# The 31-row convolution of one core's decoder step in 16 parts of 512 instead of 8 of 1024

## The chip, the core and the metric

The kernel runs on one core of a Trainium2 chip. The core has five engines that follow lists of instructions of their own and wait for each other by semaphores: TensorE (PE, with its weight loads shown apart as PEld), VectorE (DVE), ScalarE (ACT), GpSimd (POOL) and SyncE (SP), which here only issues transfers. [...] The metric is the time of one execution on the device in microseconds (us), as a median of runs.

## What is computed

Two layers of a decoder trunk for a prompt of 2048 tokens and 8 single-step samples, D_MODEL = 1024. The change lies in the even layer's branch A, a causal depthwise convolution of 31 rows over 512 channels, which follows a gated product of the input projection:

```python
def causal_depthwise_conv(x, buf, w):
    k_len, ch = w.shape
    xp = jnp.concatenate([buf.astype(x.dtype), x], axis=1)
    y = lax.conv_general_dilated(xp, w.astype(x.dtype)[:, None, :], window_strides=(1,), padding='VALID',
                                 dimension_numbers=('NWC', 'WIO', 'NWC'), feature_group_count=ch)
    return y, xp[:, xp.shape[1] - (k_len - 1):]
...
    p = h @ w_in
    glu_val, glu_gate, gate_a, qkv, z, beta_l, a_l = jnp.split(p, EVEN_SPLITS, axis=-1)
    c, conv_buf_new = causal_depthwise_conv(glu_val * jax.nn.sigmoid(glu_gate), conv_buf, dw_w)
    c = jax.nn.silu(layer_norm(c + dw_b.astype(c.dtype), ln_g, ln_b))
    a_out = c * jax.nn.silu(gate_a)
    qkv_c, qkv_buf_new = causal_depthwise_conv(qkv, qkv_buf, sc_w)
```

Branch B, a gated delta rule over q, k and v (with a short convolution of 4 rows), the output projections, memory cross attention and a second layer follow.

## The kernel before, in words

The kernel's text is a Python program that writes out the instructions of all engines in one order. The class `Flow` keeps a rough clock for each engine and for each piece of data; every wrapper (`F.mm` L160, `F.act` L176, `F.tt` L214, `F.stt` L218) adds a price to its engine's clock and issues the instruction. A dense generator makes TensorE's work; after each of its small steps `pump` lets side tasks take a step when their data are ready by the clocks (L336). `spawn` gives a task a rank: 2 for what dense work waits for soon, 1 for what it waits for later. A task of rank 1 is held back while ScalarE's or VectorE's clock is more than 3500 ns ahead of TensorE's (`LIM`, L60). The order on each engine is thus fixed before the run, by prices and not by events; an engine takes its instructions strictly in that order.

`phase1` (L650) is the input projection of the even layer. Its main part, `dense_main` (L938), takes 26 blocks of 128 output channels against five tiles of tokens (512, 512, 512, 260 and 260 columns). A group is one block against one tile: 24 matmuls into one of three PSUM banks of the pool `mm2`, then `fin_...` empties the bank. For the convolution's channels b = 0..3 a pair of blocks is run side by side: `fin_gate` (L852) writes tanh of the gate into the tile `glu` (ScalarE), `fin_val` (L862) multiplies it by the values (VectorE reads `glu` and PSUM). The blocks of q, k and v come between (`fin_qkv` L899: ScalarE empties the bank into `raw`; `conv4` L920: ScalarE makes the first product, VectorE three further ones, `qacc`, all in SBUF). The weights of a block come in two halves by SP's queue and are split into `rhi` (ScalarE or VectorE) and `rlo` (GpSimd or VectorE, by `F.ve` L207) ahead of their use; the last four blocks are z 3 and the gates sg 0..3.

`conv31` (L877) is the convolution of one half of one channel block: ScalarE makes the first product with the bias into `cacc` [128, 1024] in SBUF, VectorE adds 30 products in place, one instruction of 1024 elements a partition each (L886), two at a step. There are 8 such parts; `conv_q` lets two be open at a time and `cacc` has two places. The part is stored to DRAM by SP's queue. `dense_main` starts the gate of channel block b only when all of b - 2 is convolved (L943).

`tail` (L958) waits for the last q, k, v convolution, starts `sample_mix` (L2068, the samples' own convolutions and delta steps, rank 2, whose small matmuls go into banks of the pool `bg2`, five banks given out in turn under one tag), and when the 8 parts and the mix are done it closes their places. `places` (L1382) opens the delta rule's places once that and the second token tile of the last three blocks (`h1`) are done; then `prep` (L1102) loads the first chunks of k, q and decays. The delta rule's chain over 16 chunks follows, with products of the attention weights (`Fill`) as dense work, and then the rest of the two layers.

Of the kernel before, what the change touches and what calls it, by code (L numbers as in the profile page):

```python
# [30 lines left out]
class Pool:  # L31
    """A tile pool that notes whose place each tile takes."""
# [23 lines left out]
class Flow:  # L56
    """Engine wrappers that keep rough clocks of the engines and of the data, and the interleaving of side tasks with
    dense work by these clocks."""

    LIM = (1500.0, 3500.0, 1e9)  # L60
    # what passes from the end of an operation till another one sees its result
    VIS = {"pe": 130.0, "act": 190.0, "dve": 130.0, "pool": 110.0}

    def __init__(self, nc, tc):
        self.nc, self.tc = nc, tc
        self.rel = {}
        self.t = {"pe": 0.0, "act": 0.0, "dve": 0.0, "pool": 0.0, "sync": 0.0, "gpsimd": 0.0, "scalar": 0.0}
        self.hw = self.ring = 0.0
        self.tick, self.cold, self.cols = 0, True, 0.0
        self.cur = self.t0 = 0.0  # L70
        self.tasks = []
        # by tensor: writes and reads as (first, last partition, first, last element, time), last use, free place
        self.wr, self.rd, self.last, self.slot = {}, {}, {}, {}
        # stores that wait for their data before they join their queue: by tensor, time and arguments
        self.pend = {}
# [13 lines left out]
    def region(ap):  # L89
        a, o = ap.ap, ap.offset  # L90
        n = ap.tensor.name
        if ap.space == DRAM or a[0][0] == 0:
            # (writes to DRAM never meet earlier ones here)
            return n, -1, 1, o, o + sum((c - 1) * abs(s) for s, c in a)
# [12 lines left out]
    def ready(self, ins, outs, eng):  # L107
# [3 lines left out]
        for r in outs:  # L111
# [3 lines left out]
            # products on the same place of PSUM follow each other without a wait  # L115
# [32 lines left out]
    def pe_op(self, cost, out, lhsT, rhs):  # L148
        """the array's clock halves after a tick with too little work"""
# [38 lines left out]
    def move(self, out, in_, scale=None):  # L188
        """copy on whichever of ScalarE and VectorE is free first"""
# [8 lines left out]
    def rows(self, out, in_, f):  # L198
        """out[:, h, :] = in_[:, h, :] * f[:, h], on whichever of ScalarE and VectorE ends first"""
# [7 lines left out]
    def ve(self, n, w=0.0):  # L207
        """VectorE or GpSimdE for an operation on n elements a partition, whichever ends first"""
# [55 lines left out]
    def dma(self, out, in_, eng="sync"):  # L264
        """a transfer; it joins its queue, where each waits for the ones before it, only when its data and place are ready"""
# [41 lines left out]
    def split(self, hi, lo, src, eng="dve", scale=1.0):  # L307
        """hi + lo == src, both in float32r."""
# [4 lines left out]
    def spawn(self, gen, hi=1, front=False):  # L313
        """hi: 2 what dense work waits for soon, 1 what it waits for later, 0 what may wait"""
# [34 lines left out]
    def until(self, cond):  # L349
        """dense work: let side tasks go on till cond holds"""  # L350
# [7 lines left out]
    def run(self, dense=None):  # L358
        """Alternate dense quanta (generator) with side-task steps until the dense work ends."""
# [42 lines left out]
def rsqrt(F, pool, y, x, n, tag, eng="dve"):  # L402
    """y = x ** -0.5 on a narrow float32 tile [128, n]."""
# [11 lines left out]
def token_rstd(F, C, pool, ppool, acc, n, scale, tag):  # L415
    """acc [128, n] holds partial sums; returns [128, nc] of (sum over partitions * scale + eps) ** -0.5,
    tokens on partitions."""
# [11 lines left out]
def spread(F, C, pool, ppool, r, n, tag, dg=None):  # L429
    """r [128, nc] tokens on partitions -> psum [128, n], every partition holding the row of tokens."""  # L430
# [15 lines left out]
def mm3_steps(F, out, K, w, x):  # L446
    """generator: out += (w0 + w1)^T (x0 + x1) without the product of the two low parts."""
# [21 lines left out]
class Ring:  # L469
    """Weight blocks [128, width] in two float32r parts, in n places that are taken in turn; they are loaded in parts of  # L470
    lw columns."""

    def __init__(self, F, pool, n, raw, width=1024, lw=512, tag="r"):
# [6 lines left out]
        # where the places lie, as [pool, number], and the ring that had the first ones  # L480
        self.where, self.prev = [[pool, n]], None
        # a second pool for the parts as they come, as (pool, number, up to which block)
# [6 lines left out]
    def has(self, name, i):  # L489
        """the block is in place by the clocks"""  # L490
# [10 lines left out]
    def place(self, i):  # L501
        """the pool of a block and its places"""
# [16 lines left out]
    def load(self):  # L519
        """the next part of a block"""  # L520
# [69 lines left out]
def bc(ap, n):  # L590
    """[128, k] -> [128, k, n] with the last axis repeated"""
# [4 lines left out]
def gates(F, C, cp, tp, bgp, D, st):  # L596
    """generator: per token and head beta, the cumulated log decay in its chunk, and its exponentials"""
# [16 lines left out]
    # softplus(x) = max(x, 0) + log1p(exp(-|x|))  # L614
# [8 lines left out]
    # log1p(e) = ln(u) + (e - (u - 1)) / u  # L623
# [26 lines left out]
def phase1(F, C, I, D, st, P, R, mmp, bgp, loaders, mix, hp):  # L650
    """Input projection of the even layer with its two causal convolutions. R: the weights' places; loaders: what loads
    them, and after them the weights of what follows; mix(pool): the sample tokens. The places of h are given back
    tile by tile: the first one's, hp, are taken by what follows."""
# [7 lines left out]
    def hs(t, x, k):  # L661
        """part x of h: channels k of token tile t"""
        return h0[8 * x + k] if t == 0 else ht[t][x][:, k, :]

    # (the gates of the first half, which nothing else waits for, come last)
# [22 lines left out]
    # token tiles: x -> h, beside the memory keys and values of the first layer  # L688
    with F.tile_pool(name="x1", bufs=1, side="right") as xp:
        R.more = xp, NMORE, 33  # L690
        # the last token tile's place holds the memory till its own h comes
# [37 lines left out]
        def squares():  # L729
            """adds up the squares of each token"""  # L730
# [74 lines left out]
        def ba(t, w):  # L805
            """beta and the decays before their functions, tokens on partitions"""
# [42 lines left out]
    conv_q, cdone, qdone = Res(2), set(), set()  # L849
# [12 lines left out]
    def fin_val(b, t, n, ps):  # L862
# [6 lines left out]
        if t == 1:  # L869
            F.spawn(conv31(b, 0))  # L870
        if t == 4:
# [3 lines left out]
            F.spawn(conv31(b, 1))  # L875

    def conv31(b, u):  # L877
        yield conv_q.ok
        conv_q.take()
        g = gl[b]  # L880
        acc = ap.tile([128, 1024], F32, tag="cacc", name="cacc", bufs=2)
        o = 1024 * u
        F.act(acc, g[:, o:o + 1024], AF.Identity, scale=C.dww[:, b, 0:1], bias=C.dwb[:, b:b + 1])
        yield
        for i in range(1, 31):
            F.stt(acc, g[:, o + i:o + i + 1024], C.dww[:, b, i:i + 1], acc, ALU.mult, ALU.add)  # L886
            if i % 2 == 0:
                yield
        F.dma(D.c[b][:, o:o + 1024], acc)
        conv_q.give()  # L890
# [8 lines left out]
    def fin_qkv(b, t, n, ps):  # L899
        # b: 0..11  # L900
# [37 lines left out]
    def dense_main():  # L938
        i = 2
        for m in main[1:]:  # L940
            (kind, b), n = m[0], len(m)
            if kind == "gate" and b > 1:
                yield from F.until(lambda: (b - 2, 1) in cdone)  # L943
# [14 lines left out]
    def tail():  # L958
# [3 lines left out]
        yield lambda: len(cdone) == 8 and "mix" in st.done  # L962
# [10 lines left out]
class Pools:  # L973
    """Pools that are opened and closed one by one."""
# [13 lines left out]
class Fill:  # L988
    """The products of the attention weights with the memory: G = w_xq^T k^T g and V w_xo of each layer and head."""
# [12 lines left out]
    def begin(self):  # L1002
        """the place of the keys and values, which come from phase 1"""
# [51 lines left out]
def phase2(F, C, I, D, st, P, fill, hp, mmp, bgp, after):  # L1055
    """Gated delta rule of the even layer, beside the products of the attention weights with the memory, in chunks of 128
    tokens, four heads at a time. It starts beside the end of phase 1, whose places it takes one after the other; what
    comes after takes its places step by step. hp: the place of the first token tile's h. Returns the dense work."""
# [12 lines left out]
    def small(tag, first, n, shape=(128, 4, 128)):  # L1071
        """one of n places that the first token tile's h had"""
# [5 lines left out]
    def room(tag, n):  # L1078
        """a place for a chunk; two of them are given back early"""
# [20 lines left out]
    # The l2 norm of k stays out of the tiles: with r = 1 / |k|, T = (1 + A)^-1 = r^-1 (1 + A')^-1 r, where  # L1100
# [1539 lines left out]
```

## Time and profile before

| | us |
|---|---|
| median of 3 runs | 2962.66 (2961.9 to 2962.97) |
| span of the profiled execution, first to last instruction | 2951.0 |
| VectorE busy in the span | 1987.4 (67%) |
| TensorE busy in the span | 2737.2 (93%) |

The profile gives the profiled execution by its span alone; what lies around a span is 2962.66 - 2951.0 = 11.7 us against the median of the runs. Times inside the kernel are us from the start of the span. A row of the timeline merges like instructions that follow each other on one engine: start, length, engine, line, operation, output and inputs, count, and in brackets the idle time before it and what ended that. A line such as L222 is a wrapper's, so the name of the tile tells which step it is. [...]

### The profile page before, as it was taken

The numbers are of one execution on the slowest core, as the hardware profiler recorded it, in microseconds if no ns is written. First come the engines' busy times: TensorE is split into PE (matmuls) and PEld (weight loads), VectorE is DVE, ScalarE is ACT, GpSimd is POOL, SyncE is SP. The second block draws the span as 40 slices with busy tenths as digits, with TensorE's granted clock in tenths as the row PEclk, the third lists the DMA queues.
The fourth block names the chain that finished last, engine by engine and source line by source line (L and its number), as shares of the span: only waits on it lengthen the run. The fifth ranks groups of instructions, "written<-read, shape, count | busy, mean of one in ns | idle before, by whom it ended". The sixth has DMA issues, their size and how long they took to land.

```text
span 2951.0 us, 52358 instructions
## 1 busy us (share of the span) xinstructions
PE 2737.2 (93%) x20075; PEld 2500.1 (85%) x20075; DVE 1987.4 (67%) x4625; ACT 1023.1 (35%) x2435; POOL 667.3 (23%) x939
## 2 busy tenths in 40 slices
PE   7899999998978678899999999899999998999997
PEld 6878888887777678789989889899999898789997
DVE  6738998988547778787665565777755445765453
ACT  5532223242245455443232234444422112432321
POOL 4301102111043455212322221111011111222210
PEclk9999999999989789899999999999999999999999
DMA  7611112123355556666654533422435556421211
GB/s 239 209 46 44 53 63 65 47 79 112 116 137 159 136 155 200 198 214 205 226 164 141 176 117 103 157 72 72 164 124 164 173 175 196 150 83 60 70 62 54
DMA packets 277723, 382.08 MB, mean 129 GB/s; under 512 B 46368, under 2 KB 176736, under 8 KB 277472
## 3 DMA queue, kind: packets, MB, share of 16 engines
q1 hardware_dynamic: 256608, 311.34, 33.6%
q0 software_dynamic: 20864, 67.39, 7.3%
q8 instruction: 158, 2.59, 0.4%
q14 instruction: 93, 0.76, 0.1%
HBM read 280.57 MB, written 96.43 MB: 128 GB/s over the span
## 4 chain that ended last, share of the span: by engine, by line
PE 35%; DMA 12%; DVE 8%; issue 4%; ACT 2%; POOL 1%; SPq 1%; DVEq 0%; POOLq 0%; ACTq 0%
PE ps_mm L165 31%; DMA a_big<-d_sp 3%; DVE a_big L222 2%; DMA a_big<-d_sq 2%; DMA w_f<-d_x 1%; PE ps_bg L165 1%; DMA rraw<-d_VW 1%; PE ps_row L165 1%; POOL w_sqb L216 1%; PE ps_pt L169 1%; DVE rlo L216 1%; DMA a_big<-in_cache_v 1%; DVE xl L216 1%; DVE w_d L216 1%; SPq L305 1%
## 5 line engine op out<-in xcount | busy, mean ns | idle before, releaser
L216 POOL TENSOR_TENSOR rlo<-rraw,rhi 128x512 fp32r<-128x512 f32 x145 | 216.9, 1505 | 610.6 <-ACT rhi L183 481.7
L222 DVE SCALAR_TENSOR_TENSOR cacc<-glu,dww,cacc 128x1024 f32<-128x1024 f32 x240 | 328.0, 1379 | 5.8 <-ACT cacc L183 1.4
L216 POOL TENSOR_TENSOR w_sqb<-w_sqb,w_sqq 128x512 f32<-128x512 f32 (+1 forms) x101 | 139.2, 1378 | 652.4 <-ACT w_sqq L183 646.5
L165 PE MATMUL ps_mm<-xh,rlo 128*128 128x256 f32 (+1 forms) x1920 | 274.4, 284 | 0.0
L165 PE MATMUL ps_mm<-xh,rhi 128*128 128x256 f32 (+1 forms) x1920 | 271.8, 284 | 2.6 <-DVE pool_sm L216 2.0
L165 PE MATMUL ps_mm<-xl,rhi 128*128 128x256 f32 (+1 forms) x1920 | 271.5, 283 | 0.0
L165 PEld LDWEIGHTS ps_mm<-xh,rhi 128*128 128x128 f32 x1920 | 248.8, 191 | 5.9 <-issue 2.2
L165 PEld LDWEIGHTS ps_mm<-xh,rlo 128*128 128x128 f32 x1920 | 249.7, 192 | 1.6
L165 PEld LDWEIGHTS ps_mm<-xl,rhi 128*128 128x128 f32 x1920 | 248.0, 190 | 2.4
L165 PE MATMUL ps_mm<-hh,rhi 128*128 128x512 f32 (+2 forms) x1152 | 217.2, 330 | 20.9 <-ACT hh L183 15.7
L165 PE MATMUL ps_mm<-hl,rhi 128*128 128x512 f32 (+2 forms) x1152 | 215.7, 330 | 0.0
L165 PEld LDWEIGHTS ps_mm<-hh,rhi 128*128 128x128 f32 x1152 | 178.6, 192 | 42.9 <-ACT hh L183 16.1
L165 PE MATMUL ps_mm<-hh,rlo 128*128 128x512 f32 (+2 forms) x1152 | 214.7, 329 | 0.0
L216 DVE TENSOR_TENSOR w_y<-ps_mm,w_y 128x256 f32<-128x256 f32 (+1 forms) x248 | 103.1, 420 | 159.3 <-PE ps_mm L165 155.1
L222 DVE SCALAR_TENSOR_TENSOR a_big<-a_big 128x256 f32<-128x256 f32 x256 | 104.0, 444 | 148.7 <-DMA a_big<-d_sp 80.9
L183 ACT ACTIVATE rhi<-rraw 128x512 fp32r<-128x512 f32 x233 | 143.1, 628 | 164.4 <-DMA rraw<-d_VW 36.3
L165 PEld LDWEIGHTS ps_mm<-hl,rhi 128*128 128x128 f32 x1152 | 178.1, 192 | 17.6
L165 PEld LDWEIGHTS ps_mm<-hh,rlo 128*128 128x128 f32 x1152 | 177.0, 192 | 18.9 <-issue 1.0
L165 PE MATMUL ps_mm<-mh,rhi 128*128 128x256 f32 (+1 forms) x1152 | 170.1, 288 | 8.6 <-ACT mh L183 8.6
L165 PE MATMUL ps_mm<-ml,rhi 128*128 128x256 f32 (+1 forms) x1152 | 170.7, 290 | 3.1 <-DVE ml L216 3.1
L165 PE MATMUL ps_mm<-mh,rlo 128*128 128x256 f32 (+1 forms) x1152 | 163.6, 283 | 0.0
L165 PEld LDWEIGHTS ps_mm<-mh,rhi 128*128 128x128 f32 x1152 | 153.5, 195 | 11.2 <-ACT mh L183 9.5
(426 smaller groups left out, 5360.1 us busy)
## 6 DMA issues: line engine op xcount, KB each, us to landing
w_f<-d_x SPq DMA_DIRECT2D x60, 512.0 KB
d_x<-w_y SPq DMA_DIRECT2D x44, 512.0 KB
w_y<-d_x SPq DMA_DIRECT2D x44, 512.0 KB
a_big<-in_cache_k POOLq DMA_DIRECT2D x64, 256.0 KB, 4.1
a_big<-in_cache_v POOLq DMA_DIRECT2D x64, 256.0 KB, 4.1
rraw<-in_w_in SPq DMA_DIRECT2D x56, 256.0 KB
d_qkv<-so SPq DMA_DIRECT2D x48, 256.0 KB
rraw<-in_w_xk SPq DMA_DIRECT2D x32, 256.0 KB
```

Source lines behind the costliest of these rows:

```text
L165: self.nc.tensor.matmul(out, lhsT, rhs, start=start, stop=stop)
L169: self.nc.tensor.transpose(out, in_, ident)
L183: self.nc.scalar.activation(out=out, in_=in_, func=func, scale=scale, **kw)
L216: self._e(eng).tensor_tensor(out=out, in0=a, in1=b, op=op)
L222: self._e(eng).scalar_tensor_tensor(out=out, in0=a, scalar=s, in1=b, op0=op0, op1=op1, **kw)
L305: getattr(self.nc, eng).dma_start(out=out, in_=in_)
```

## The change

The convolution of a channel block is cut into four parts of 512 tokens, 16 in all, each started when the token tile that ends it has come (tiles 0, 1, 2, and 4 for the last). Parts whose number 4b + u leaves 2 when divided by 3 (numbers 2, 5, 8, 11 and 14) are `alone`: ScalarE makes each of the 30 products into one of two places `pm`, and GpSimd adds them to `pacc`, two at a step, one such part open at a time (`conv_p`). The other 11 keep VectorE's fused instruction with 512 elements, four at a step, but the running sum lies in a PSUM bank of the pool `bg2`, and only the last of the 30 writes to SBUF (`cacc`, now one place of 512). Stores are 16 of 256 KB where 8 of 512 KB were. The two conditions on convolved parts name all four parts. The rest of the diff empties comment lines.

```diff
-    conv_q, cdone, qdone = Res(2), set(), set()
+    conv_q, conv_p, cdone, qdone = Res(2), Res(1), set(), set()
...
-        if t == 1:
-            F.spawn(conv31(b, 0))
+        if t in (0, 1, 2, 4):
+            F.spawn(conv31(b, min(t, 3)))
...
-            F.spawn(conv31(b, 1))
...
-        yield conv_q.ok
-        conv_q.take()
...
+        alone = (4 * b + u) % 3 == 2
+        q = conv_p if alone else conv_q
+        yield q.ok
+        q.take()
         g = gl[b]
-        acc = ap.tile([128, 1024], F32, tag="cacc", name="cacc", bufs=2)
-        o = 1024 * u
-        F.act(acc, g[:, o:o + 1024], AF.Identity, scale=C.dww[:, b, 0:1], bias=C.dwb[:, b:b + 1])
-        yield
+        o = 512 * u
+        if alone:
+            acc = ap.tile([128, 512], F32, tag="pacc", name="pacc", bufs=1)
+        else:
+            acc = bgp.tile([128, 512], F32, tag="bg", name="ps_cv")
+        F.act(acc, g[:, o:o + 512], AF.Identity, scale=C.dww[:, b, 0:1], bias=C.dwb[:, b:b + 1])
+        yield
+        ms = []
         for i in range(1, 31):
-            F.stt(acc, g[:, o + i:o + i + 1024], C.dww[:, b, i:i + 1], acc, ALU.mult, ALU.add)
-            if i % 2 == 0:
+            out = acc
+            if alone:
+                m = ap.tile([128, 512], F32, tag="pm", name="pm", bufs=2)
+                F.copy(m, g[:, o + i:o + i + 512], scale=C.dww[:, b, i:i + 1])
+                ms.append(m)
+                if i % 2 == 0:
+                    for m in ms:
+                        F.tt(acc, acc, m, ALU.add, eng="pool")
+                    ms.clear()
+                    yield
+                continue
+            if i == 30:
+                out = ap.tile([128, 512], F32, tag="cacc", name="cacc", bufs=1)
+            F.stt(out, g[:, o + i:o + i + 512], C.dww[:, b, i:i + 1], acc, ALU.mult, ALU.add)
+            if i % 4 == 0:
                 yield
-        F.dma(D.c[b][:, o:o + 1024], acc)
-        conv_q.give()
+        F.dma(D.c[b][:, o:o + 512], out)
+        q.give()
         cdone.add((b, u))
...
-                yield from F.until(lambda: (b - 2, 1) in cdone)
+                yield from F.until(lambda: cdone >= {(b - 2, u) for u in range(4)})
...
-        yield lambda: len(cdone) == 8 and "mix" in st.done
+        yield lambda: len(cdone) == 16 and "mix" in st.done
```

## Rows read from the trace of the kernel before

**Rows 1.** The page's busy times of the whole span: engine, us, share, instructions.
```profile
PE 2737.2 (93%) x20075; PEld 2500.1 (85%) x20075; DVE 1987.4 (67%) x4625; ACT 1023.1 (35%) x2435; POOL 667.3 (23%) x939
```
**Rows 2.** Windows: the stretch; then its length and the busy time of PE, PEld, DVE, ACT and POOL with their counts; the granted clock; the share of the transfer engines; GB/s.
```profile
195.00:760.00 565.00, 548.24 (x2930) 473.11 (x2929) 495.16 (x558) 154.56 (x294) 87.52 (x64) 0.98 0.21 68
785.00:1290.00 505.00, 406.64 (x4338) 365.68 (x4337) 354.22 (x1066) 259.30 (x840) 188.17 (x372) 0.86 0.59 163
```
**Rows 3.** TensorE's waits from 195 to 700 us: who waited, for whom, us in total, times, the longest.
```profile
PE ps_mm L165 <- DVE glu L222: 5.2, 2, 2.8
PE ps_mm L165 <- ACT raw L183: 2.4, 2, 1.5
```
**Rows 4.** TensorE's waits from 700 to 800 us, same columns.
```profile
PE ps_cs L165 <- DVE m_sq L216: 6.3, 1, 6.3
...
PE ps_ks L165 <- DVE m_S L216: 1.3, 2, 0.7
```
**Rows 5.** Timeline of VectorE from 318 us, ahead of the first stop of TensorE in rows 3, and from 699 us, ahead of the one in rows 4.
```profile
318.31 12.66 DVE L222 SCALAR_TENSOR_TENSOR cacc<-glu,dww,cacc 128x1024 f32<-128x1024 f32 x10
330.89 0.68 DVE L222 SCALAR_TENSOR_TENSOR glu<-glu,ps_mm 128x512 f32<-128x512 f32 x1
...
701.77 6.01 DVE L222 SCALAR_TENSOR_TENSOR cacc<-glu,dww,cacc 128x1024 f32<-128x1024 f32 x4
...
709.67 2.50 DVE L222 SCALAR_TENSOR_TENSOR cacc<-glu,dww,cacc 128x1024 f32<-128x1024 f32 x2
...
712.38 0.23 DVE L216 TENSOR_TENSOR m_sq<-m_s 128x64 f32<-128x64 f32 x1
```
**Rows 6.** Timeline of TensorE: two undisturbed runs of 8 matmuls at 251 us, and the stretch behind the stop at 706 us.
```profile
251.44 1.98 PE L165 MATMUL ps_mm<-hh,rhi 128*128 128x512 f32 x8
253.25 1.98 PE L165 MATMUL ps_mm<-hl,rhi 128*128 128x512 f32 x8
...
713.11 3.76 PE L165 MATMUL ps_mm<-hl,rhi 128*128 128x512 f32 x8
716.67 2.95 PE L165 MATMUL ps_mm<-hh,rlo 128*128 128x512 f32 x8
719.46 2.00 PE L165 MATMUL ps_mm<-hh,rhi 128*128 128x512 f32 x8
```
**Rows 7.** Windows around that stop, columns as in rows 2.
```profile
710.00:720.00 10.00, 7.34 (x21) 5.91 (x22) 9.48 (x20) 0.29 (x1) 0.00 (x0) 0.56 0.13 53
720.00:730.00 10.00, 10.00 (x63) 8.75 (x62) 5.56 (x12) 4.07 (x6) 0.00 (x0) 1.00 0.21 69
```
**Rows 8.** The hand-over to the delta rule, three timelines: TensorE behind the second token tile of the last three blocks, VectorE's last instruction of the mix and its next one, SP's first load of `prep`.
```profile
780.25 1.98 PE L165 MATMUL ps_mm<-hh,rlo 128*128 128x512 f32 x8
782.07 1.98 PE L165 MATMUL ps_mm<-hh,rhi 128*128 128x512 f32 x8
...
778.95 1.12 DVE L222 SCALAR_TENSOR_TENSOR m_S<-ps_vb,m_kq,m_S 128x128 f32<-128x128 f32 x4
792.62 0.69 DVE L216 TENSOR_TENSOR dec<-zeros,dec 128x512 f32<-128x512 f32 x1 [12.55 <-DMA dec<-d_gc]
...
783.50 0.37 SPq L305 DMA_DIRECT2D k<-d_qkv  x1
```
**Rows 9.** Groups of instructions by shape from 195 to 760 us: line, engine, operation, tiles, shape, count; busy us and mean ns; idle us before them.
```profile
L222 DVE SCALAR_TENSOR_TENSOR cacc<-glu,dww,cacc 128x1024 f32<-128x1024 f32 x240 | 328.0, 1379 | 5.8 <-ACT cacc L183 1.4
L222 DVE SCALAR_TENSOR_TENSOR qacc<-raw,scw,qacc 128x512 f32<-128x512 f32 x144 | 117.0, 812 | 28.7 <-ACT qacc L183 25.3
L222 DVE SCALAR_TENSOR_TENSOR glu<-glu,ps_mm 128x512 f32<-128x512 f32 x12 | 8.2, 682 | 15.2 <-PE ps_mm L165 15.2
L183 ACT ACTIVATE qacc<-raw,scw 128x512 f32<-128x512 f32 x48 | 34.8, 725 | 148.4 <-DVE raw L235 137.9 <-POOL raw L251 10.0
L183 ACT ACTIVATE cacc<-glu,dwb,dww 128x1024 f32<-128x1024 f32 x8 | 9.9, 1241 | 40.0 <-DMA d_c<-cacc 23.2 <-DVE glu L222 16.8
L216 POOL TENSOR_TENSOR rlo<-rraw,rhi 128x512 fp32r<-128x512 f32 x46 | 85.7, 1876 | 450.1 <-ACT rhi L183 384.1 <-DVE rhi L235 45.2 <-PE ps_mm L165 20.3
```
**Rows 10.** Instructions of the tiles `rlo` (from 195 to 760 us) and `cacc`: count; shortest, median and longest ns; first and last start.
```profile
L216 POOL TENSOR_TENSOR rlo<-rraw,rhi x46: 1279/1904/2280, 244.3 to 734.3; 128x512 fp32r<-128x512 f32 x46
...
L305 SPq DMA_DIRECT2D d_c<-cacc x8: 319/352/423, 312.7 to 750.6; - x8
```
**Rows 11.** VectorE and GpSimd at the same time, from the timelines: a triple of `qacc` without GpSimd and one beside it; a read of PSUM beside GpSimd.
```profile
463.57 2.32 DVE L222 SCALAR_TENSOR_TENSOR qacc<-raw,scw,qacc 128x512 f32<-128x512 f32 x3
...
641.34 3.25 DVE L222 SCALAR_TENSOR_TENSOR qacc<-raw,scw,qacc 128x512 f32<-128x512 f32 x3 [0.85 <-ACT qacc L183]
641.90 1.35 POOL L216 TENSOR_TENSOR rlo<-rraw,rhi 128x512 fp32r<-128x512 f32 x1 [2.01 <-ACT rhi L183]
...
448.02 4.38 POOL L216 TENSOR_TENSOR rlo<-rraw,rhi 128x512 fp32r<-128x512 f32 x2 [35.56 <-ACT rhi L183]
448.94 0.42 DVE L222 SCALAR_TENSOR_TENSOR glu<-glu,ps_mm 128x260 f32<-128x260 f32 x1
```
**Rows 12.** Timeline: VectorE's last gated product of the last channel block, and TensorE's first two matmuls into a bank of `bg2` for the mix.
```profile
571.37 0.41 DVE L222 SCALAR_TENSOR_TENSOR glu<-glu,ps_mm 128x252 f32<-128x252 f32 x1
...
712.66 0.69 PE L165 MATMUL ps_cs<-m_sq,ones 128*128 128x64 f32 x2 [6.27 <-DVE m_sq L216]
```

## The prediction, as it was put on record

> **What bounds the kernel now.** I began with the busy times of the whole span: TensorE 93%, VectorE 67%, GpSimd 23% [rows 1]. The first question is then whether VectorE sets the time anywhere. The convolution's stores are issued from 312.7 to 750.6 us [rows 10], so I asked for the windows of that stage: from 195 to 760 us VectorE is busy 495.2 of 565 us (88%), ScalarE 154.6, GpSimd 87.5, but TensorE 548.2 (97%) at a granted clock of 0.98 [rows 2]. Both are near full; which one ends last is read from TensorE's waits. Up to 700 us it stops for only 5.2 us for VectorE's gated product and 2.4 us for ScalarE's copy of a bank [rows 3]; after that once for 6.3 us and twice for 1.3 us in all, for VectorE's part of the samples' mix [rows 4]. VectorE's list shows why: ten convolution instructions of 12.66 us stand ahead of the gated product at 330.89, and six stand ahead of or between the steps that make `m_sq` [rows 5]. The kernel's clocks price one of them at 1024 / 0.96 + 130 = 1197 ns and the trace has a mean of 1379 [rows 9], so VectorE runs behind the order that was written for it. [...] The 16 matmuls from 713.11 to 719.46 take 6.35 us, where two runs of 8 at full clock take 2 x 1.81 = 3.62, so 2.7 us more [rows 6].
>
> The stage's end is TensorE's too: the delta rule's first load is issued at 783.50, 1.4 us behind the second token tile of the last blocks (782.07); the mix ended at 780.1 [rows 8], and the convolution some 30 us before that [rows 10]. From 785 to 1290 us no engine is full (TensorE 406.6 of 505, VectorE 354.2) [rows 2]: that is a chain of chunks that begins with this load. So the path runs through TensorE's order up to about 782 us and then through the chain; the convolution lies on it only by the stops above.
>
> **The change part by part.** *VectorE.* Removed: 240 instructions of 1024 elements, 328.0 us [rows 9]. Added: 11 x 30 = 330 of 512 elements with the sum in PSUM. No row has such an operation with its output in PSUM. The nearest row reads one operand from SBUF and one from PSUM at the same size, 682 ns [rows 9]; above it lies the form with all operands in SBUF, 812 ns, waits included [rows 9]; below it half of the shortest spacing seen, 12.66 / 10 / 2 = 633 ns [rows 5]. That is 330 x 0.633 = 209, x 0.682 = 225, x 0.812 = 268 us. I take 225, so VectorE loses 103 us (60 to 119). The kernel's clocks price it at 663 ns, for once close to the row.
>
> [...]
>
> *GpSimd and the common cost of two operands.* Five parts give GpSimd 150 additions of 512. The nearest row is `rlo`: mean 1876 ns, from 1279 to 2280 [rows 9, 10]; 192 to 342 us in all. The spread has a visible cause. A triple of `qacc` takes 2.32 us alone and 3.25 with one GpSimd addition inside it; that addition takes 1.35, two others take 4.38 together; a VectorE operation that reads PSUM keeps its 0.42 us beside GpSimd [rows 11]. So two operands in SBUF cost both engines time, and one in PSUM costs none. Before, VectorE's two-operand work was 328 + 117 of 565 us (79%); after it is the 117 of `qacc` (21%). The share of the surplus 1876 - 1279 = 597 goes with it: 1279 + 597 x 21 / 79 = 1.44 us, which I take: 216 us, and GpSimd rises from 87.5 to about 300 of 565. In return up to 48 triples of `qacc` grow by 3.25 - 2.32 = 0.93: 0 to 45 us, I take 30. VectorE ends at 495 - 103 + 30 = 422 us (75%; 376 to 480). `rlo` shares GpSimd, but is made a block (over 20 us of matmuls) ahead of its use; cover enough for one or two waiting pairs of 2.9 us.
>
> *ScalarE.* 150 products at the price of its first products for `qacc`, 725 ns [rows 9]: 109 us; the 16 first products at half of 1241 and some more instead of 8: about 2 us more. ScalarE goes from 154.6 to 266 of 565 us (47%). Behind a product that waits for a place `pm` stand the copies that empty TensorE's banks. Also new: the wait of `pacc` and of `cacc`, now one place each, for their store. For `cacc` 23.2 us of ScalarE's time went that way in the stage before, in which no stop of TensorE of that kind shows [rows 3, 9]; I cost it at nothing, and at 5 us if two parts end together.
>
> *SP.* Eight more stores at 0.35 us each [rows 10], 2.8 us over 560, on a queue that is not on the path; the bytes are the same.
>
> *TensorE.* No instruction changes. What can go is 5.2 + 6.3 + 1.3 us of stops on VectorE [rows 3, 4] and the 2.7 us of slow clock behind one: 15.5 us. With VectorE at 75% its list no longer holds ten instructions ahead of a gated product, and the convolution is over before the mix begins: the last channel block's product is done at 571 us [rows 12], the parts then still open are at most three of 30 x 0.682 = 20 us, at three quarters of VectorE some 80 us together, so about 650. What is late next is ScalarE, whose 2.4 us [rows 3] I leave standing, with 2.5 us of new stops for the products' sake (0 to 8; the upper end is three times the stops there now). Sum: -15.5 + 2.5 = -13 us at 782 us, carried through the chain. Against 2951.0 + 11.7 around the span this is 2950 us.
>
> **The rivals.** *Hidden anyway.* TensorE's stops go, but the chain from 785 us begins on loads and on a mixture of dense work, and the order behind it is written anew; or VectorE gains little because a sum in PSUM costs 0.81 us, in which the change would not do what it says. For it: TensorE was 97% busy, and the gain is a handful of stops. Against it: the chain's first load follows TensorE's tile by 1.4 us. Then 3 us are left: 2960.
>
> *Slower: ScalarE waits behind GpSimd.* The kernel's clocks give a pair of additions 2 x (512 x 2.1 + 160) = 2.47 us; with the first product (0.61), the passing of the results (0.3) and half a step of dense work (0.45) a pair of products follows every 3.8 us. On the chip a pair needs 0.73 + 0.1 + 2a, where a is one addition. Up to a = 1.49 us that fits. Above, ScalarE falls behind by 2 (a - 1.49) each pair, and with it the banks. One group of 24 matmuls (5.4 us by rows 6) is slack once for each of the five parts, 27 us. At a = 1.876, the row's mean, the loss is 150 x 0.386 - 27 = 31 us, against the 15.5 gained: 2978. It outweighs the gain from a = 1.77 us on. For it: the mean before. Against it: that mean stands beside VectorE's two-operand work, which falls to a quarter.
>
> [...]
>
> *A bank held too long.* The mix takes its banks in turn from the same five. If a sum still lay in one when the mix asked at about 700 us [rows 12], TensorE would stand until that part's end, up to 20 us: 2965. Some 50 us of room speak against it.
>
> *More than that.* The chain's start might gain by an emptier VectorE, and the copies by ScalarE: twice the forecast, 2937.
>
> **How the numbers follow.** Forecast (13 us gained; own range 2943 to 2956): 0.50. More than that: 0.08. Hidden: 0.22. ScalarE behind GpSimd: 0.16. The bank: 0.04. A measurement of this kernel tells about 0.2%, 6 us, from no change. Faster than that are the forecast and its double, 0.58; within it the hidden case, 0.22; slower the last two in the main, 0.20. For 8 in 10 the range reaches from 2932, below the double, to 2979, the upper case at the row's mean; it takes in VectorE's and GpSimd's bounds, since both act through those two cases.
>
> **What would show it.** In the profile of the changed kernel: VectorE's instructions with the sum in PSUM at 0.63 to 0.72 us, undisturbed beside GpSimd; VectorE at 376 to 480 us of the stage; additions `pacc` at 1.3 to 1.5 us; no wait of TensorE for `glu` or `m_sq` and a clock near 1.00 around the mix; the first load of k about 13 us before 783.5; the convolution over by about 650 us. Against me: additions at 1.8 us or more, ScalarE waiting for GpSimd by more than 30 us with TensorE waiting for `raw` or `glu` behind it, or a delta rule that starts earlier and ends at the same time as before.

## The result and the profile after

The changed kernel takes 2985.1 us (median of 4 runs, 2978.93 to 2988.1) beside 2962.28 us for the kernel before in the same comparison: ratio 1.0082, interval 1.0068 to 1.0096. It is 0.8% slower; the forecast was 0.4% faster. The time also lies above the upper end of the range, 2979.

First the busy times of the whole span, then windows of the stage of the convolution, of its stretch from 600 to 700 us and of the delta rule (columns as in [rows 2]).

```profile
PE 2742.9 (92%) x20075; PEld 2505.2 (84%) x20075; DVE 1946.2 (65%) x4716; ACT 1124.5 (38%) x2600; POOL 847.5 (28%) x1084
```
```profile
195.00:760.00 565.00, 540.75 (x2893) 463.94 (x2892) 480.08 (x707) 252.66 (x449) 262.53 (x204) 0.98 0.21 68
600.00:700.00 100.00, 85.20 (x444) 73.16 (x443) 86.25 (x119) 53.61 (x93) 52.69 (x39) 0.94 0.28 89
...
785.00:1290.00 505.00, 395.60 (x4238) 355.58 (x4237) 327.38 (x1033) 255.15 (x836) 186.61 (x369) 0.83 0.56 155
```

Against [rows 2], VectorE fell by 15 us only (480.1 for 495.2), ScalarE and GpSimd rose by 98 and 175 us, and TensorE did less in the same 565 us. From 600 to 700 us it is busy 85.2, at a granted clock of 0.94 (of TensorE's full one); the kernel before has in that stretch:

```profile
600.00:700.00 100.00, 99.06 (x548) 86.52 (x547) 91.95 (x109) 34.65 (x63) 14.65 (x10) 1.00 0.28 93
```

The waits of TensorE in the changed kernel from 195 to 760 us:

```profile
PE ps_mm L165 <- ACT raw L183: 8.7, 5, 4.2
PE ps_cs L165 <- POOL pacc L216: 7.4, 1, 7.4
PE ps_mm L165 <- DVE glu L222: 2.7, 2, 2.0
PE ps_mm L165 <- ACT so L183: 2.7, 2, 1.8
```

The wait for `glu` halved against [rows 3], but the waits for ScalarE's copies of banks grew from 2.4 to 11.4 us, and the stop for the mix of [rows 4] is there still (7.4 for 6.3; the profile names GpSimd, and the timeline below shows `m_sq` as the late one). The groups by shape, columns as in [rows 9]:

```profile
L222 DVE SCALAR_TENSOR_TENSOR ps_cv<-glu,dww,ps_cv 128x512 f32<-128x512 f32 x319 | 238.5, 754 | 13.0 <-ACT ps_cv L183 4.5
L216 POOL TENSOR_TENSOR pacc<-pacc,pm 128x512 f32<-128x512 f32 x150 | 210.0, 1400 | 169.0 <-ACT pm L183 161.1
L222 DVE SCALAR_TENSOR_TENSOR qacc<-raw,scw,qacc 128x512 f32<-128x512 f32 x144 | 153.3, 1068 | 30.0 <-ACT qacc L183 26.6
...
L183 ACT ACTIVATE pm<-glu,dww 128x512 f32<-128x512 f32 x150 | 102.7, 715 | 32.2 <-POOL pacc L216 32.1
...
L222 DVE SCALAR_TENSOR_TENSOR cacc<-glu,dww,ps_cv 128x512 f32<-128x512 f32 x11 | 8.2, 748 | 0.4
```

And by tile: count; shortest, median, longest ns; first and last start.

```profile
L222 DVE SCALAR_TENSOR_TENSOR ps_cv<-glu,dww,ps_cv x319: 741/756/758, 214.1 to 668.1; 128x512 f32<-128x512 f32 x160
L222 DVE SCALAR_TENSOR_TENSOR qacc<-raw,scw,qacc x144: 739/752/1785, 252.7 to 672.0; 128x512 f32<-128x512 f32 x144
...
L216 POOL TENSOR_TENSOR pacc<-pacc,pm x150: 1262/1298/1787, 267.7 to 713.8; 128x512 f32<-128x512 f32 x150
...
L305 SPq DMA_DIRECT2D d_c<-pacc x5: 319/320/425, 360.4 to 720.0; - x5
```

Three things are to be seen. A sum in PSUM, where TensorE's products (`ps_mm`) land too, takes 754 ns, not 682, and never more than 758. `qacc`, with all in SBUF, has the same median but reaches 1785. And the five parts of ScalarE and GpSimd, one open at a time, are stored from 360.4 to 720.0 us, some 90 us apart ((720.0 - 360.4) / 4): VectorE was done with its parts at 669, but the convolution runs on into the samples' mix, whose first step on VectorE starts at 676. Number 11, stored at 636.4, runs ahead of the mix, beside the last `qacc`; number 14 runs beside its first 44 us. There the timelines of VectorE, ScalarE, GpSimd and TensorE read so:

```profile
678.48 0.89 DVE L235 COPY m_S<-m_sg 128x8 f32<-128x8 f32 x1 [1.70 <-DMA m_S<-in_state_conv_a]
...
680.18 0.98 DVE L235 COPY m_S<-m_sg 128x8 f32<-128x8 f32 x1
...
693.77 1.28 DVE L229 TENSOR_SCALAR m_s<-m_s 128x96 f32<-128x96 f32 x1
...
696.48 1.28 DVE L216 TENSOR_TENSOR m_sq<-m_s 128x64 f32<-128x64 f32 x1
...
682.78 0.72 ACT L183 ACTIVATE pm<-glu,dww 128x512 f32<-128x512 f32 x1 [0.90 <-POOL pacc L216]
683.41 0.58 ACT L183 ACTIVATE so<-ps_mm 128x512 f32<-128x512 f32 x1
...
679.83 11.60 POOL L216 TENSOR_TENSOR pacc<-pacc,pm 128x512 f32<-128x512 f32 x8 [0.50 <-ACT pm L183]
693.72 5.30 POOL L216 TENSOR_TENSOR pacc<-pacc,pm 128x512 f32<-128x512 f32 x4 [2.29 <-ACT pm L183]
...
684.04 5.51 PE L165 MATMUL ps_mm<-h,rhi 128*128 128x512 f32 x16 [1.78 <-ACT so L183]
...
697.86 0.66 PE L165 MATMUL ps_cs<-m_sq,ones 128*128 128x64 f32 x2 [7.40 <-POOL pacc L216]
```

A copy of 8 elements takes nearly 1 us (0.17 in the kernel before), and `m_sq` 1.28 us where [rows 5] has 0.23, all beside GpSimd's additions. A copy of a bank (`so`) stands behind a product that waited for GpSimd, and TensorE waits for that copy. The hand-over, TensorE's second token tile and SP's first load, with the first product of the output projection and the first of the second layer's map (`zh`) as later marks:

```profile
790.90 1.98 PE L165 MATMUL ps_mm<-hh,rhi 128*128 128x512 f32 x8
...
792.18 0.39 SPq L305 DMA_DIRECT2D k<-d_qkv  x1
...
L165 PE MATMUL ps_mm<-xh,rlo x150: 277/283/472, 1282.0 to 1399.9; 128*128 128x256 f32 x86, 128*128 128x264 f32 x64
...
L165 PE MATMUL ps_mm<-zh,rhi x128: 276/279/467, 1912.7 to 2155.6; 128*128 128x256 f32 x112, 128*128 128x264 f32 x16
```

The same two marks of the kernel before:

```profile
L165 PE MATMUL ps_mm<-xh,rlo x192: 274/283/567, 1261.5 to 1395.2; 128*128 128x256 f32 x128, 128*128 128x264 f32 x64
...
L165 PE MATMUL ps_mm<-zh,rhi x128: 276/280/580, 1883.0 to 2123.6; 128*128 128x256 f32 x112, 128*128 128x264 f32 x16
```

The load still follows TensorE's tile by 1.3 us (1.4 in [rows 8]), but 8.7 us later than before's 783.50. Then the loss grows: 20.5 us at the first mark, 29.7 at the second. The convolution is long over there, and no instruction of that work was changed. These marks come from one execution each, and before's was a short one: its span lies 32.8 us under the changed kernel's (2983.8 - 2951.0), the medians only 22.8 apart. So some 10 us of the 29.7 belong to that execution, and sizes are taken from medians below.

### The profile page after: what moved, and what is told of

The parts are those of the page before. It is cut to its first block, busy times and chain, and to the rows that moved or that the text cites. A ratio compares the mean times of both kernels' runs of the same rounds, so it can differ in the third digit from the quotient of the medians.

```text
span 2983.8 us, 52928 instructions
## 1 busy us (share of the span) xinstructions
PE 2742.9 (92%) x20075; PEld 2505.2 (84%) x20075; DVE 1946.2 (65%) x4716; ACT 1124.5 (38%) x2600; POOL 847.5 (28%) x1084
## 4 chain that ended last, share of the span: by engine, by line
PE 49%; DVE 18%; DMA 13%; issue 5%; ACT 4%; POOL 2%; SPq 2%; DVEq 0%; ACTq 0%; POOLq 0%
PE ps_mm L165 42%; DVE ps_cv L222 4%; DVE qacc L222 4%; PE ps_bg L165 3%; SPq L305 2%; DMA a_big<-d_sq 2%; DMA a_big<-d_sp 2%; DVE a_big L222 1%; DMA rraw<-d_VW 1%; DVE w_d L216 1%; DMA a_big<-in_cache_k 1%; DMA d_VW<-gv 1%; PE ps_pt L169 1%; PE ps_row L165 1%; PE ps_bg L169 1%
## 5 line engine op out<-in xcount | busy, mean ns | idle before, releaser
L216 POOL TENSOR_TENSOR rlo<-rraw,rhi 128x512 fp32r<-128x512 f32 x137 | 184.1, 1351 | 261.1 <-ACT rhi L183 192.7
L216 POOL TENSOR_TENSOR pacc<-pacc,pm 128x512 f32<-128x512 f32 x150 | 210.0, 1400 | 169.0 <-ACT pm L183 161.1
L222 DVE SCALAR_TENSOR_TENSOR ps_cv<-glu,dww,ps_cv 128x512 f32<-128x512 f32 x319 | 238.5, 754 | 13.0 <-ACT ps_cv L183 4.5
L222 DVE SCALAR_TENSOR_TENSOR qacc<-raw,scw,qacc 128x512 f32<-128x512 f32 x144 | 153.3, 1068 | 30.0 <-ACT qacc L183 26.6
```

The source lines that it names most:

```text
L216: self._e(eng).tensor_tensor(out=out, in0=a, in1=b, op=op)
L222: self._e(eng).scalar_tensor_tensor(out=out, in0=a, scalar=s, in1=b, op0=op0, op1=op1, **kw)
```

## The experiments

Three theories. **Theory 1:** the parts of ScalarE and GpSimd, above all the last two (number 11 ahead of the mix, number 14 beside it), make TensorE late at the hand-over. **Theory 2:** the order behind the hand-over, written anew from the kernel's own clocks, is worse by itself, whatever the convolution does. **Theory 3:** the bank given to a sum, or the finer parts, cost the time.

**All 16 parts on VectorE.**
```diff
-        alone = (4 * b + u) % 3 == 2
+        alone = False
```


> All 16 parts take VectorE's way with the sum in a PSUM bank; no product of ScalarE and no addition of GpSimd is left in the convolution. Theory 1 (the five parts of ScalarE and GpSimd make TensorE wait for bank copies and for the mix): the waits for raw and for m_sq go; VectorE gets 480 sums at 0.754 = 362 us in place of 328, so it stays near 530 of 565 us and some of the stops of before for glu and m_sq come back; 2958 to 2970 us. Theory 2 (the order of the delta rule's stage is written anew and is worse by itself): the stage from the first load of k to the first product of the output projection stays about 11 us longer than before's 478 us, and the time 2972 to 2982 us. Theory 3 (the bank given to a sum, or the finer parts, are what costs): 2980 us or more.

2984.3 us, ratio 1.0091 (1.0073 to 1.011). TensorE's one wait from 195 to 760 us, `qacc`, then SP's first load and VectorE's last step of the mix:
```profile
PE ps_gc L165 <- DVE g L231: 1.5, 1, 1.5
```
```profile
L222 DVE SCALAR_TENSOR_TENSOR qacc<-raw,scw,qacc 128x512 f32<-128x512 f32 x144 | 118.5, 823 | 31.6 <-ACT qacc L183 28.1
```
```profile
804.43 0.37 SPq L305 DMA_DIRECT2D k<-d_qkv  x1
...
802.21 0.25 DVE L222 SCALAR_TENSOR_TENSOR m_o<-m_o,dn,m_zs 128x32 f32<-128x32 f32 x1
```
No stop of TensorE is left but one of 1.5 us, and `qacc` is back at before's mean; so these did come with ScalarE's and GpSimd's parts. But VectorE is now behind with the convolution (last store at 776.3) and the mix (802), and the hand-over waits for the mix, not for TensorE. None of the theories had said that (Theory 3's number is met, but not by its cause, as the next kernel shows): VectorE alone can't carry 16 such parts in this stage in time. From the load to the output projection it is 469.0 us (1273.4 - 804.43), less than before's 478, where Theory 2 had put 11 more: so its order, a new one again, cost nothing up to there in that execution.

**The same, with the sum in SBUF.**
```diff
-            acc = bgp.tile([128, 512], F32, tag="bg", name="ps_cv")
+            acc = ap.tile([128, 512], F32, tag="cacc", name="cacc", bufs=2)
```
(and all 30 in place.)


> As the kernel with all 16 parts on VectorE, but the sum lies in SBUF (two places of 512), no bank is used. It tells a sum in PSUM from a sum in SBUF: 0.754 us was measured in PSUM; half of the instruction of 1024 is 0.690, the row of the short convolution in SBUF has 0.812. Theory 1: 2958 to 2970 us, as with the bank. Theory 2: the stage from the first load of k to the output projection differs from before's by some 10 us either way, as its order is again another. Theory 3: at least 5 us less than with the bank.

3032.42 us, ratio 1.0257 (1.0236 to 1.0278); first load at 826.64.
```profile
L222 DVE SCALAR_TENSOR_TENSOR cacc<-glu,dww,cacc x480: 652/752/1869, 214.5 to 813.9; 128x512 f32<-128x512 f32 x160
```
The same tile in the kernel before, with 1024 elements:
```profile
L222 DVE SCALAR_TENSOR_TENSOR cacc<-glu,dww,cacc x240: 1184/1284/2402, 225.9 to 746.7; 128x1024 f32<-128x1024 f32 x120
```
No theory had this time. Theory 3 falls for the bank: without it, it is worse. Undisturbed the two forms are alike (median 752 in SBUF, 756 in PSUM), but in SBUF the longest is 1869 and the mean 803, in PSUM 754. The finer cut does cost: two of 752 ns for one of 1024 with a median of 1284 are 0.22 us more a pair.

**Parts 2, 5 and 8 alone on ScalarE and GpSimd.**
```diff
+        alone = 4 * b + u in (2, 5, 8)
```


> Of the five parts of ScalarE and GpSimd the numbers 11 and 14, which ran beside the samples' mix, go to VectorE; 2, 5 and 8 stay. Theory 1: the stop for m_sq and the bank copies of 600 to 750 us get shorter, the ones from 400 to 500 us stay: the first load of k comes some 4 to 8 us earlier than at 792.2, 2972 to 2980 us. Theory 2: whatever happens ahead of that load, the stage behind it is some 10 us longer than before's: 2975 to 2985 us. Theory 3: no change, 2985 us.

2957.96 us, ratio 0.9995 (0.9979 to 1.001), first load at 769.87: 22.3 us earlier than with the two late parts, more than Theory 1 had asked for, and 13.6 us earlier than before. (Of the two, only number 14 had run beside the mix.) The time is less than any theory had, 2972 or more. Yet it is before's: the gain over before is gone later.

**Before, with another order behind the hand-over.**
```diff
         P.close("m2", "a1")
+        F.t["pe"] += 2500.0
         st.done.add("tail")
```


> The kernel before, its convolution and all work ahead of the delta rule untouched; only the kernel's own clock of TensorE is set 2500 ns on where the samples' mix is done, so that the order of the delta rule's stage is written anew (no instruction is added or left out). Theory 1: 2960 us, give or take 4. Theory 2: the time moves by 8 to 20 us, with nothing changed in the stage of the convolution.

2983.02 us, ratio 1.009 (1.0062 to 1.0117), 25 us more with the convolution of before.
```profile
780.28 0.37 SPq L305 DMA_DIRECT2D k<-d_qkv  x1
```
```profile
L165 PE MATMUL ps_mm<-xh,rlo x160: 274/283/467, 1277.8 to 1399.6; 128*128 128x256 f32 x96, 128*128 128x264 f32 x64
```
The first load is no later than before's, the output projection is 16 us later. Theory 2 holds, with more than the 8 to 20 us that it had, and in size it is as much as the whole result.

**Convolution and order apart.** At the hand-over the kernel's own clocks are the same in both kernels but for TensorE's, which stands at 691358 ns in before and at 692338 in the changed kernel (written by the program as it makes its list), and the kernel's model of TensorE's clock depends on that absolute number. So the number that this model sees can be set at the hand-over as it is in the other kernel; from there on the lists of all engines are the same, instruction by instruction.
```diff
         yield lambda: st.done >= {"h1", "tail"}
+        F.off, F.tick, F.cold, F.cols = 691358.2029743594 - F.t["pe"], 202, False, 4148.428800000001
```
(`pe_op` adds `F.off` where its model looks at the clock; the other three are the model's counts. For before with the changed kernel's order the numbers are 692337.8076410254 and 6741.1968000000015.) The changed kernel with before's order, the kernel with early parts alone with before's order, and before with the changed kernel's order:

> The changed kernel, with the convolution as it is; only the kernel's own model of TensorE's clock is set at the hand-over to the delta rule to the state that it has there in the kernel before. The order of all engines behind the hand-over is then that of before, instruction by instruction. Theory 1 (the late parts of ScalarE and GpSimd cost at the hand-over): first load of k still near 792, all behind it as in before, so before's time and 8.7 us: 2967 us (2963 to 2971). Theory 2 (the order behind is the greater part of the loss): also well under 2985, by 12 to 20 us. Against both: 2985 us, if the loss were of the convolution alone and went on behind the hand-over.

> The kernel with only parts 2, 5 and 8 on ScalarE and GpSimd, and behind the hand-over the order of the kernel before, in the same way. Its first load of k came at 769.9, 13.6 us ahead of before's. If a gain at the hand-over is carried through the chain, as the prediction had it: 2945 us (2941 to 2950). If the rest of the time were set by something else (loads, the samples' attention): 2956 us or more.

> The kernel before, convolution untouched, with the changed kernel's order behind the hand-over. First load of k near 783. Theory 2: the changed kernel's time less its 8.7 us at the hand-over, 2972 to 2980 us. Theory 1 alone: 2958 to 2962 us, as before.

In that order: 2965.87 us, ratio 1.0035 (1.0021 to 1.0049); 2945.27 us, 0.9969 (0.9953 to 0.9986); 2972.44 us, 1.0058 (1.0037 to 1.0079). All three came out as expected. First loads, in the same order, with the window from 600 to 700 us of the second of them:
```profile
792.91 0.39 SPq L305 DMA_DIRECT2D k<-d_qkv  x1
```
```profile
770.64 0.37 SPq L305 DMA_DIRECT2D k<-d_qkv  x1
```
```profile
600.00:700.00 100.00, 100.00 (x555) 87.56 (x554) 90.86 (x138) 35.16 (x64) 12.67 (x11) 1.00 0.30 94
```
```profile
779.53 0.37 SPq L305 DMA_DIRECT2D k<-d_qkv  x1
```
With GpSimd at 12.7 us of these 100 in place of 52.7, TensorE is busy all of them at a clock of 1.00. The convolution of this second kernel is not over before the mix either. VectorE's last sums, now with parts 11 and 14:
```profile
L222 DVE SCALAR_TENSOR_TENSOR cacc<-glu,dww,ps_cv x13: 747/748/749, 250.4 to 710.2; 128x512 f32<-128x512 f32 x13
```

The marks of these runs, one profiled execution each; "to map" is the first product of `zh` less the first load:

| convolution | order behind | first load, us | to map, us | map to end, us | ratio |
|---|---|---|---|---|---|
| before | before | 783.5 | 1099.5 | 1068.0 | 1 |
| changed | before | 792.9 | 1099.3 | 1067.8 | 1.0035 |
| early parts alone | before | 770.6 | 1106.8 | 1070.6 | 0.9969 |
| before | changed | 779.5 | 1126.0 | 1073.4 | 1.0058 |
| changed | changed | 792.2 | 1120.6 | 1071.1 | 1.0082 |
| early parts alone | its own | 769.9 | 1117.2 | 1069.8 | 0.9995 |
| before | 2500 ns on | 780.3 | 1134.3 | 1067.8 | 1.009 |

The column "to map" goes by the order and hardly by the convolution: 1099 to 1107 us with before's, 1117 to 1134 with three others. What follows the map takes 1068 to 1073 us in all seven. The kernel with all parts on VectorE has a fifth order and 1107.5 (1911.9 - 804.43), so not every other order costs as much. A single execution strays: before's lies some 10 us under its median, that of before with the changed order 8 us above (2980.91 for 2972.44), and three with before's convolution have the first load at 779.5, 780.3 and 783.5. The ratios, from medians, are the measure of an order's price.

**What of the late parts costs.** Three kernels with the changed convolution and before's order; in parts 11 and 14 the additions go to VectorE, the products are left out, or the additions are left out:
```diff
-                        F.tt(acc, acc, m, ALU.add, eng="pool")
+                        F.tt(acc, acc, m, ALU.add, eng="pool" if 4 * b + u < 9 else "dve")
```
```diff
+            if alone and 4 * b + u > 9 and i > 2:
+                F.tt(acc, acc, m, ALU.add, eng="pool")
...
+                continue
```
```diff
+                    if 4 * b + u > 9 and i < 30:
...
+                        continue
                     for m in ms:
```


> The changed kernel with before's order behind the hand-over, and the additions of the two late parts (11 and 14) made by VectorE; ScalarE still makes their 60 products. It tells what of the late parts costs. If it is GpSimd beside VectorE's short steps of the samples' mix (m_S copies 0.8 to 1.2 us in place of 0.2, m_sq 1.28) and ScalarE's wait for GpSimd: first load of k near 772 to 778, 2950 to 2956 us. If it is ScalarE's products ahead of the bank copies: first load near 790, 2965 us. VectorE gets some 60 x 0.6 = 36 us more; if it is full by then, a wait for glu shows, and the time is in between.

> The changed kernel with before's order behind the hand-over; in the two late parts (11 and 14) ScalarE makes only the first two products, and GpSimd adds the second of them 29 times, at the pace of the changed kernel. So 56 products are left out, those two parts of the output are not the convolution, and ScalarE waits for GpSimd no more there. If the late parts cost by GpSimd beside VectorE's short steps: first load of k stays near 793, a stop of TensorE for the samples' m_sq near 7 us stays, 2964 to 2968 us. If they cost by ScalarE waiting for GpSimd with bank copies and the mix's exponentials behind it: near 772, no such stop, 2946 to 2950 us.

> The twin: in the late parts ScalarE makes all products, and 56 of GpSimd's 60 additions are left out (those parts of the output are not the convolution). If the late parts cost by GpSimd, in either way: first load of k near 770 to 774 and 2945 to 2950 us, as with the additions on VectorE. If by ScalarE's products ahead of its copies and the changes of its table between products and exponentials: near 785 to 793, 2958 to 2966 us.

The first: 2949.32 us, ratio 0.9979 (0.9967 to 0.9991), first load at 772.16. VectorE's 60 additions took 739 ns each in the mean (the 0.6 us expected is the kernel's price, 512 / 0.96 + 68 = 601 ns), and TensorE's waits for `raw` fell to 3.0 us. The second: 2976.91 us, 1.0059 (1.0044 to 1.0074), first load at 796.47; ScalarE no longer waits for GpSimd in those parts, and it is worse, not better, and worse than either reading had it. TensorE's two largest waits and GpSimd's timeline:
```profile
PE ps_cs L165 <- issue: 13.2, 1, 13.2
PE ps_mm L165 <- ACT raw L183: 11.1, 6, 4.1
```
```profile
670.00 31.15 POOL L216 TENSOR_TENSOR pacc<-pacc,pm 128x512 f32<-128x512 f32 x21
```
GpSimd, which no product holds up now, adds without a pause until 701 us, and the stop for `m_sq` grows to 13.2 us (the profile names no engine for it). The third: 2950.12 us, 0.9976 (0.9961 to 0.9992), first load at 772.83, with all of ScalarE's products still there.
```profile
600.00:700.00 100.00, 95.89 (x515) 82.05 (x513) 72.73 (x146) 59.63 (x102) 11.96 (x10) 0.98 0.34 104
```
In all three the order ahead of the hand-over is drawn anew as well, as the parts' prices change. But the second and the third are twins: TensorE's list is the same in both from the first instruction to the last. VectorE in the second, then in the third:
```profile
670.04 5.21 DVE L222 SCALAR_TENSOR_TENSOR qacc<-raw,scw,qacc 128x512 f32<-128x512 f32 x3
...
677.54 0.60 DVE L229 TENSOR_SCALAR m_sg<-m_sg 128x32 f32<-128x32 f32 x1 [0.59 <-ACT m_sg L183]
...
702.94 0.23 DVE L216 TENSOR_TENSOR m_sq<-m_s 128x64 f32<-128x64 f32 x1
```
```profile
664.15 0.18 DVE L229 TENSOR_SCALAR m_sg<-m_sg 128x32 f32<-128x32 f32 x1 [3.73 <-ACT m_sg L183]
...
680.59 0.23 DVE L216 TENSOR_TENSOR m_sq<-m_s 128x64 f32<-128x64 f32 x1
```
Without the additions `m_sq` comes 22.4 us earlier (680.59 for 702.94), and the first load 23.6. Of the 22.4, 13.4 are there when the mix starts (`m_sg`, 664.15 for 677.54): the triple of `qacc` that [rows 11] has at 2.32 us takes 5.21 beside the additions (3.51 in the third kernel, beside `rlo`), and TensorE waits 11.1 us for `raw`, for 5.2 without them. The other 9 are lost in the mix's steps. So it is GpSimd's additions beside VectorE's work, `qacc` first and then the short steps of the mix, not ScalarE's products, not the changes of its table (the third kernel has six of them from 660 to 690 us, 1.28 us each) and not its wait. Numbers 11 and 14 were moved together in every kernel, so what each costs alone is not shown.

## Why the prediction failed, step by step

**What bounds: right.** TensorE ends last, and the delta rule's first load follows its tile by 1.3 us. With before's order a shift of that load reaches the end: 13 us earlier gave 12.3 us (2957.54 - 2945.27), 9.4 later gave 8.3 (2965.87 - 2957.54). A mark is good to some 4 us, so the near agreement is partly luck.

**"The convolution is over before the mix begins ... so about 650": the first step that failed.** I gave the open parts VectorE's pace, 20 us each. A part of ScalarE and GpSimd takes some 90 us, of which 42 are additions (210.0 / 5) and 32 GpSimd's wait for products (161.1 / 5), and five in a row end at 720 us. The step "What can go is 5.2 + 6.3 + 1.3 us of stops ... and the 2.7 us of slow clock" (granted 0.56 from 710 to 720 us and 1.00 in the next ten, [rows 7]) hung on it: TensorE lost 8.7 us at the hand-over where I had it gain 13. But the late end is not by itself what costs: with numbers 11 and 14 on VectorE the convolution ends at 711 us, beside the mix too, and the first load comes at 770.6, 12.9 us ahead of before. The term that I had at nothing for TensorE is GpSimd's additions beside VectorE's last `qacc` and the mix: 23.6 us between the twins. That 12.9 meets my 13 is luck as far as "over by 650" goes.

**"Two operands in SBUF cost both engines time": the right mechanism, applied to too little.** I charged it to `qacc` alone; that came out at 153.3 - 117.0 = 36 us for 30 forecast. But I counted it as VectorE's busy time, not as a delay of TensorE behind `raw`, and the mix's copies and short steps pay it too, up to 1.1 us each, on a chain for which TensorE waits. What TensorE lost from 600 to 700 us is 14.8 us of busy time (100.00 - 85.20; before 0.9) and 6% of its clock.

**VectorE's sum in PSUM: mis-sized, 0.754 for 0.682 us.** I took the gated product as the nearest row. Its factor is a number in the instruction; the convolution's is a column of a tile, as `qacc`'s is, whose triple in [rows 11] gives 2.32 / 3 = 0.77. That the factor makes the difference was not tried apart. The relief was 328.0 - 238.5 - 8.2 = 81 us, not 103; inside the range given, but with the surplus of `qacc`, longer steps of the mix and more of the mix inside the window little of it is left (480 us, the upper bound of 376 to 480). The place of the sum by itself made 4 ns: medians of 756 in PSUM and 752 in SBUF, the latter in the kernel with all parts there.

**"Carried through the chain": the second step that failed.** I took the order behind the hand-over as given and named its rewriting only inside the rival "Hidden anyway", as a loss of what was gained. It has a price of its own: 14.9 us by the change's order with before's convolution (2972.44 - 2957.54), 12.7 with the early parts by theirs (2957.96 - 2945.27), 25 us by another. With the hand-over's 8.3 us the first makes 23.2 us, and the result is 22.8 (2985.1 - 2962.28). Why one order is worse was not taken apart, and that cause stays open. What the traces show is where: the six kernels with before's order take 477 to 484 us from the first load to the output projection and 621 to 625 from there to the map, the two with the changed order 490 and 493, then 631 and 633. From 785 to 1290 us the granted clock is 0.86 to 0.88 with before's order and 0.83 and 0.84 with the changed one; whether that is cause or consequence is not shown.

**What held.** Additions of 1.40 us (1.44 forecast), 210 us in all (216), products of 715 ns (725), sums in PSUM undisturbed beside GpSimd (758 ns at most), the banks (no wait of TensorE for one shows).

**The rivals.** "ScalarE waits behind GpSimd" had the right side and nearly the time, 2978, but not the cause: additions of 1.40 us lie below its point of 1.49 (the 0.1 us in it, from a product to its addition, stood on no row; the changed kernel has 0.13, a product of 0.72 us from 678.98 and its addition at 679.83), ScalarE's wait of 32.1 us is there, and taking it away in the late parts did not help. Its sign, more than 30 us of that wait with TensorE waiting for `raw`, was met all the same; it does not tell this rival from the cause that was found. "Hidden anyway" had a piece of the cause with no price of its own. The 11.7 us around the span were mostly the profiled execution being a short one (the changed kernel has 2985.58 - 2983.8 = 1.8); the sum starts from the median either way.

The fastest version is the one with parts 2, 5 and 8 alone on ScalarE and GpSimd and before's order: 0.3% faster than before. The change's idea was sound; the last two of its five parts stood on GpSimd beside work that TensorE waits for, and the list behind was drawn anew.

## What to carry to other kernels

Where the order is written by a planner's clocks, any edit draws it anew for all that follows: hold the order behind the edit fixed, or try the new order with the old code, before the time is put down to the edit. Work given to GpSimd is to be asked for its end, not only for its sum: a slow lane that takes parts one by one may still run when a chain of VectorE steps begins for which TensorE waits. Price an instruction by a row with the same kind of operands, the factor included.

## What the runs showed of the hardware

Beside GpSimd's additions a VectorE copy of one operand from SBUF, 8 elements wide, took 0.89 and 0.98 us (0.17 without them, in the third of the last kernels), while sums with one operand in PSUM never took more than 758 ns in 319; in the kernel with all 16 sums in SBUF, whose GpSimd has no such additions but `rlo`, the longest was 1869. The short steps show it most: `m_s` at 693.77, right behind the start of an addition at 693.72, takes 1.28 us, about as long as an addition (1.30 at the median), where the same step takes 0.20 in the third of the last kernels. Why the two engines hold each other up was not shown. And GpSimd's own `rlo`, with a median of 1904 ns in [rows 10], took 1298 in the changed kernel, where the convolution's sums on VectorE no longer have both operands in SBUF.
